# An inference step of a hybrid decoder: the MLP's instructions kept in traced order on four engines, and its last chunk widened to three pairs

## The chip, the cores and the metric

The kernel runs on one core of one Trainium2 chip. The metric is the device time of one execution, in microseconds (us). Three runs of the kernel before took 2996.69, 2999.52 and 3004.34 us; their median is 2999.52 us. The core has five engines with a queue each: TensorE (PE, matmuls; PEld is its weight load), VectorE (DVE), ScalarE (ACT), GpSimd (POOL) and SyncE (SP, which here only starts DMA transfers). ACT starts some transfers too.

## The reference

Two layers, each a mixer and then an MLP, on 1024 prompt tokens and 8 decode tokens (1032 columns), all in float32. The change touches only the MLP, which both layers run:

```python
def _conv_ffn(xn, w_up, conv_w, conv_b, w_down, conv_state):     # xn: (tokens, 1024), normed
    gpre, up = jnp.split(xn @ w_up, 2, axis=-1)                  # 2816 gate and 2816 inner columns
    full = jnp.concatenate([conv_state.astype(gpre.dtype), gpre], axis=1)
    acc = conv_b + full[:, 0:t] * conv_w[0]
    for j in range(1, CONV_W):                                   # CONV_W = 3 taps along the tokens
        acc = acc + full[:, j:j + t] * conv_w[j]
    h = jax.nn.gelu(acc) * up
    return h @ w_down, full[:, full.shape[1] - (CONV_W - 1):]
```

The result is added to the residual; the next layer (or the last norm) follows.

## The kernel before, in words

Activations lie transposed: features on 128 partitions, the 1032 token columns along the row. A float32 operand is split into a rounded high part and a low rest (`parts`, L442), and a product is three matmuls: high by high, high by low, low by high.

Both matrix products of the MLP use a Strassen-like scheme: one 2 x 2 block product needs seven block products instead of eight, with sums on both sides. `seven` (L484) runs one such round: products 0 to 6 accumulate in three double PSUM banks in the order a b c a b c b, so product 3 needs the bank of product 0 read out, product 4 that of 1, product 5 that of 2, product 6 that of 4, and product 1 of the next round that of product 6. Each product takes its weight factor from `factors` (L446): POOL forms the sums of weight blocks (L467 to L473), ACT writes the high part (L459) and a copy in PSUM (L461), DVE subtracts for the low part (L462). Four factors are kept ahead; their split tiles are four, so factor S+4 reuses the tile of factor S.

`climb` (L570) is the up-projection: 22 rounds, f = 0 to 21, each 7 products of 24 matmuls (128 x 258 columns). A round makes 128 gate and 128 inner columns. `after(i, pt)` reads out product i: ACT copies product 0 (L600), DVE reads out products 1 (L603), 2 (L612), 3 (L595), 4 (L614), 5 (L618) and 6 (L616). POOL finishes the gate row (L593, L594, L622 to L625). `convolve` then does the three taps (ACT L629, DVE L632 four times), the GELU (ACT L634, L635) and the gating (DVE L637, twice). Round f's `convolve` is called in round f+1, after product 0. `turn` splits the seven block sums of a pair of rounds (ACT L443, DVE L444, POOL L435 to L439) and stores them in DRAM (`hid`, SP L650), 11 pairs in layer 0 and 9 in layer 1. In layer 1 the last four rounds go to DRAM unsplit (`raw`), and are multiplied after the MLP.

Round 0 is special: `first` makes the split sums of the input as its products need them, and the norm's factor `rstd` is made beside it (`make_rstd`, L221).

`descend` (L681) is the down-projection. It takes the pairs in chunks: two pairs at a time, then a single pair, then two pairs. For each chunk, j = 0 to 3 runs one round of seven products, of 6 matmuls per pair, and adds them to the accumulators `big` (L714; ACT L712 in chunk 0). `load_factors` (L559) brings a chunk's pairs from `hid`, on SP for chunk 0 and on ACT later. In chunks 1 and 2, the residual `res` is loaded through one buffer `sq_t` (SP L728), scaled (POOL L729) and added (POOL L730). In the last chunk, product 0 is read out to a buffer `t` and added by POOL to three accumulators (L718), DVE scales by `rstd` (L707), and the squares for the next norm are made (ACT L736, POOL L204).

What sets the order: each engine has one queue and runs it front to back. A scheduler of the programming framework decides at build time in which order the instructions stand in each queue, from priorities and its own estimate of what is ready; it may put a later instruction of the source ahead of an earlier one.

Of the kernel before, what the change touches and what calls it, by code (L numbers as in the profile page):

```python
# [8 lines left out]
F32 = mybir.dt.float32  # L9
# [9 lines left out]
T = 1024  # L19
# [51 lines left out]
class Trunk:  # L71
# [149 lines left out]
    def make_rstd(self, bank, std=None, tmp=None):  # L221

        nc = self.nc
        tmp = self.vec.tile([128, TT], F32, name="sq_t") if tmp is None else tmp
        parts = []
# [4 lines left out]
        if std is not None:  # L230
            nc.scalar.copy(std, tmp)
        self.rsqrt(self.rstd, tmp)
        if std is not None:
            nc.gpsimd.tensor_tensor(std, std, self.rstd, op=OP.mult)

    def rsqrt(self, out, x):
# [5 lines left out]
        nc.scalar.activation(out, out, AF.Exp, scale=-0.5)  # L242
        nc.vector.tensor_tensor(x, x, out, op=OP.mult)
# [202 lines left out]
    def factors(self, srcs, kt, mixed=False):  # L446
# [6 lines left out]
        (a11, a12), (a21, a22) = ((r[:, ::2], r[:, 1::2]) if mixed else (r[:, :kt], r[:, kt:]) for r in raws)  # L453

# [11 lines left out]
        s1, s2 = (ext.tile([128, 4, 128], F32, name=x, bufs=1)[:, :kt] for x in ("s1", "s2"))  # L466
        nc.gpsimd.tensor_tensor(s1, a21, a22, op=OP.add)  # L467
        nc.gpsimd.tensor_tensor(s2, s1, a11, op=OP.subtract)
        yield parts(s2)
        yield parts(s1)  # L470
        nc.gpsimd.tensor_tensor(a11, a11, a21, op=OP.subtract)
        yield parts(a12)
        nc.gpsimd.tensor_tensor(a12, a12, s2, op=OP.subtract)  # L473
        yield parts(a11)
# [3 lines left out]
    def factor_stream(self, units):  # L478

        units = list(units)  # L480
        next(units[0])
# [5 lines left out]
    def seven(self, pp, stream, rhs, after):  # L487

        nc = self.nc
        banks = {}
        for i, x in enumerate("abcabcb"):
            while len(self.ahead) < 4:
                nxt = next(stream, None)
                if nxt is None:
                    break
                self.ahead.append(nxt)
            hi, lo = self.ahead.popleft()
            new = x not in banks  # L500
            if new:
                banks[x] = pp.tile([128, 2, 512], F32, name=f"pp{x}", bufs=1)
            pt, right = banks[x][:, :, :QW], rhs(i)
            for k, r in enumerate(right):
                for n, (w, part) in enumerate(((hi, 0), (hi, 1), (lo, 0))):
                    for q in range(2):
                        nc.tensor.matmul(pt[:, q], w[:, k], r[:, part, q, :QW], start=(new and k == 0 and n == 0),  # L507
                                         stop=(k == len(right) - 1 and n == 2), skip_group_check=True)
            after(i, pt)

    def ffn(self, l, last):
# [11 lines left out]
        chunks = [(p, p + 1) for p in range(0, NP - 3, 2)] + [(NP - 3,), (NP - 2, NP - 1)]  # L523
# [11 lines left out]
        with self.tp(name="fpp", bufs=1, space=PSUM) as pp, self.tp(name="fpm", bufs=2, space=PSUM) as self.ps:  # L535
            self.climb(l, stream, pp, right, tu, chunks, hid, raw, NP)
            self.descend(l, last, stream, pp, tu, chunks, hid)
        pools.pop().__exit__(None, None, None)
        if last:
            with self.tp(name="fin", bufs=1) as fin:  # L540
                y = [fin.tile([128, TT], F32, name=f"y{i}") for i in range(4)]
                parts = []
                for k in range(4):
                    nc.sync.dma_start(y[k], raw[k])
                    nc.gpsimd.tensor_tensor(y[k], y[k], self.rstd, op=OP.mult)
# [6 lines left out]
        if not last:  # L552
            self.open_x()
            self.order = PAIRS
            for m in PAIRS:
                nc.scalar.activation(self.xh[m], big[:, m], AF.Copy)  # L556
                nc.vector.tensor_tensor(self.xl[m], big[:, m], self.xh[m], op=OP.subtract)

# [7 lines left out]
    def climb(self, l, stream, pp, right, tmp, chunks, hid, raw, pairs):  # L566
# [12 lines left out]
        inner, tail = {}, lambda: None  # L579
# [4 lines left out]
        def up(f):  # L584
# [3 lines left out]
            c11 = x = None  # L588

            def begin():  # L590
                if f == 0:
# [1617 lines left out]
```

## Time and profile before

| | |
|---|---|
| median of 3 runs | 2999.52 us |
| profiled execution, its own time | 2999.0 us |
| its span in the trace | 2997.3 us |
| busy share of the span | PE 92%, PEld 83%, DVE 63%, ACT 46%, POOL 37% |
| mean granted TensorE clock | 0.97 of full speed |
| chain that ended last, by engine | PE 47%, DVE 16%, POOL 11%, DMA 9%, issue 8%, ACT 8% |

The span holds, in order: mixer 0 (to 879 us), MLP 0 (to 1673 us), mixer 1 (to 2174 us), MLP 1 (to 2920 us) and the tail. Busy time of PE counts a matmul to its modelled end, so neighbours overlap; what a product costs is read from the distance of two starts.

### The profile page before, as it was taken

What the parts mean: (1) busy time and instruction counts of PE and PEld (TensorE: products, weight loads), DVE (VectorE), ACT (ScalarE), POOL (GpSimd) and SP (SyncE); (2) the same over time, 40 slices, a digit from 0 to 9 for tenths busy, and PEclk for the clock granted to TensorE, in tenths of its full rate; (3) what the DMA queues carried; (4) which work ended last, traced back from release to release, by engine and by line L of the source; (5) the groups of instructions that cost most, each with busy time, mean ns of one, the idle gap of its engine ahead of it and who ended that gap; (6) DMA issues with size and microseconds to landing.
All of it is one profiled execution on the core that took longest, in us unless ns stands there. A gap on an engine that the chain in (4) does not pass through costs nothing.

```text
span 2997.3 us, 49791 instructions
## 1 busy us (share of the span) xinstructions
PE 2761.6 (92%) x19363; PEld 2480.8 (83%) x19363; DVE 1895.8 (63%) x3187; ACT 1364.4 (46%) x2653; POOL 1123.3 (37%) x1114
## 2 busy tenths in 40 slices
PE   8999999999998999988889799999989999999798
PEld 7885545877898898988789789989978898998787
DVE  6566764456557777776458744445387777764586
ACT  4344433334445555555435423324365555555344
POOL 3621234321254444444454511110534444433554
PEclk9999999998999999999899999999989999999998
DMA  6621002521122343346674212221314333357632
GB/s 180 187 60 43 22 1 71 190 92 44 44 92 82 121 143 129 119 144 247 233 233 144 51 43 59 62 76 31 106 46 144 127 121 128 123 194 253 195 92 100
DMA packets 300911, 342.68 MB, mean 114 GB/s; under 512 B 34253, under 2 KB 246324, under 8 KB 300612
## 3 DMA queue, kind: packets, MB, share of 16 engines
q1 hardware_dynamic: 269948, 238.97, 25.0%
q10 hardware_dynamic: 21000, 66.98, 6.3%
q0 software_dynamic: 9728, 33.56, 3.3%
q8 instruction: 153, 2.51, 0.3%
q14 instruction: 82, 0.67, 0.1%
HBM read 241.13 MB, written 102.50 MB: 115 GB/s over the span
## 4 chain that ended last, share of the span: by engine, by line
PE 47%; DVE 16%; POOL 11%; DMA 9%; issue 8%; ACT 8%; ACTq 0%; SPq 0%; POOLq 0%; DVEq 0%
PE ps L284 13%; PE ppb L507 4%; PE ppc L507 3%; DVE big L632 3%; DMA sq_t<-res 3%; PE ppa L507 3%; PE pp L284 2%; PE ps L1314 2%; PE pd L284 2%; POOL s L467 2%; DMA hid<-big 2%; POOL big L622 2%; PE ps L791 1%; DMA wr<-in_ffn_w_up_dram 1%; ACT ps L461 1%
## 5 line engine op out<-in xcount | busy, mean ns | idle before, releaser
L507 PE MATMUL ppb<-s,wl 128*128 128x258 f32 x2304 | 315.8, 289 | 38.3 <-DVE big L614 10.8
L507 PE MATMUL ppb<-s,wh 128*128 128x258 f32 x2304 | 310.0, 289 | 30.2 <-DVE tu L603 25.9
L507 PEld LDWEIGHTS ppb<-s,wl 128*128 128x128 f32 x2304 | 294.2, 194 | 50.1 <-ACT wl L459 28.4
L507 PEld LDWEIGHTS ppb<-s,wh 128*128 128x128 f32 x2304 | 293.4, 195 | 36.6 <-ACT big L443 27.6
L461 ACT COPY ps<-wr 128x512 f32<-128x512 f32 (+2 forms) x440 | 205.3, 468 | 137.1 <-DVE wl L462 49.1
L507 PE MATMUL ppc<-s,wh 128*128 128x258 f32 x1536 | 217.0, 295 | 53.0 <-ACT wh L459 16.4
L507 PEld LDWEIGHTS ppc<-s,wh 128*128 128x128 f32 x1536 | 202.1, 199 | 61.1 <-ACT wl L459 27.9
L632 DVE SCALAR_TENSOR_TENSOR big<-big 128x524 f32<-128x524 f32 x176 | 185.5, 1094 | 94.7 <-ACT big L629 94.7
L284 PE MATMUL ps<-xh,wh 128*128 128x344 f32 x960 | 222.2, 336 | 12.7 <-ACT xh L556 12.7
L507 PE MATMUL ppc<-s,wl 128*128 128x258 f32 x1536 | 210.1, 290 | 19.8 <-DVE big L714 7.7
L507 PE MATMUL ppa<-s,wh 128*128 128x258 f32 x1536 | 209.6, 290 | 16.2 <-ACT st L712 8.2
L507 PEld LDWEIGHTS ppc<-s,wl 128*128 128x128 f32 x1536 | 197.3, 195 | 24.7 <-ACT wl L459 9.1
L462 DVE TENSOR_TENSOR wh<-ps,wh 128x512 fp32r<-128x512 f32 (+2 forms) x308 | 166.1, 539 | 80.9 <-ACT ps L461 54.4
L284 PE MATMUL ps<-xl,wh 128*128 128x344 f32 x960 | 214.2, 326 | 1.8 <-DVE xl L187 1.8
L462 DVE TENSOR_TENSOR wl<-ps,wl 128x512 fp32r<-128x512 f32 (+2 forms) x308 | 165.8, 538 | 76.0 <-ACT ps L461 46.4
L507 PEld LDWEIGHTS ppa<-s,wh 128*128 128x128 f32 x1536 | 197.7, 196 | 19.3 <-ACT st L712 8.4
L271 POOL TENSOR_TENSOR wr<-wr,gains 128x1024 f32<-128x1024 f32 (+1 forms) x44 | 84.3, 1915 | 338.3 <-DMA wr<-in_odd_w_in_dram 196.4
L284 PE MATMUL ps<-xh,wl 128*128 128x344 f32 x960 | 210.6, 325 | 0.0
L507 PE MATMUL ppa<-s,wl 128*128 128x258 f32 x1536 | 200.7, 283 | 2.5 <-DVE wl L462 0.8
L507 PEld LDWEIGHTS ppa<-s,wl 128*128 128x128 f32 x1536 | 190.7, 190 | 4.5 <-DVE wl L462 1.2
L284 PEld LDWEIGHTS ps<-xh,wh 128*128 128x128 f32 x960 | 161.5, 190 | 19.1 <-ACT xh L556 12.9
L467 POOL TENSOR_TENSOR s<-wr 128x512 f32<-128x512 f32 (+2 forms) x88 | 90.0, 1023 | 231.5 <-ACT wh L459 93.6
(773 smaller groups left out, 6026.6 us busy)
## 6 DMA issues: line engine op xcount, KB each, us to landing
s<-hid ACTq DMA_DIRECT2D x112, 520.0 KB
wr<-in_ffn_w_up_dram SPq DMA_DIRECT2D x88, 512.0 KB
hid<-big SPq DMA_DIRECT2D x76, 520.0 KB
hid<-st SPq DMA_DIRECT2D x57, 520.0 KB
wr<-in_ffn_w_down_dram SPq DMA_DIRECT2D x80, 256.0 KB
s<-hid SPq DMA_DIRECT2D x28, 520.0 KB
wr<-in_odd_w_in_dram SPq DMA_DIRECT2D x24, 512.0 KB
wr<-in_even_w_in_dram SPq DMA_DIRECT2D x18, 512.0 KB
```

The source lines that it names most:

```text
L271: self.gain_eng.tensor_tensor(raw, raw, gain[:, :, None].to_broadcast([128, kt, m]), op=OP.mult)
L284: nc.tensor.matmul(outs[g], l[:, kw, :], r[k][:, g * GW:(g + 1) * GW], start=(n == 0 and i == 0), stop=(n == kt - 1 and i == 2))
L461: nc.scalar.copy(pt, x)
L462: nc.vector.tensor_tensor(lo, pt, hi, op=OP.subtract)
L467: nc.gpsimd.tensor_tensor(s1, a21, a22, op=OP.add)
L507: nc.tensor.matmul(pt[:, q], w[:, k], r[:, part, q, :QW], start=(new and k == 0 and n == 0), stop=(k == len(right) - 1 and n == 2), skip_g ...
L622: p.tensor_tensor(g[:, 2 + HW:2 + T], u2[:, :T - HW], self.rstd[:, HW:T], op=OP.mult)
L632: v.scalar_tensor_tensor(cv[:, c], g[:, n + c.start:n + c.stop], taps[:, at:at + 1], cv[:, c], op0=OP.mult, op1=OP.add)
L791: nc.tensor.matmul(pt, l[:, k, :], r[k][:, s], start=(k == 0 and i == 0), stop=(k == n - 1 and i == 2))
L1314: nc.tensor.matmul(po[64 * g:64 * g + 64], v[:, kb, 64 * g:64 * g + 64], p[:, g * 512:(g + 1) * 512], start=first, stop=last)
```

## The change

The MLP's instructions on PE, DVE, ACT and POOL are tied, each to the one before it on its engine in the traced (source) order, by dependencies that need no semaphore. SP is not tied. The source is laid out anew to suit: an `agenda` holds steps for each product, and `seven` runs them after the read-out (late = 0) or after the next weight factor (late = 1). Factor S+4 is made behind product S. The taps, GELU and gating of a round are spread over products 0 to 4 of the next round; the seven turns of a pair over fifteen products; the norm over round 0. POOL's first two weight sums of a unit move two products ahead. In `descend` the chunks end with one of three pairs, whose product 0 runs twice, into banks a and b, so that it is not read out alone; POOL's three adds of `t` move to the chunk before. The last chunk's third pair is loaded behind the products of the chunk before. In layer 1, `rstd` multiplies the unsplit rounds before they are stored. Cut to its core (`...` marks what is left out):

```diff
+    @contextmanager
+    def ordered(self):
+        traced = self.nc.cur_bb.bb.instructions
+        head = traced[-1]
+        yield
+        start = next(k for k in reversed(range(len(traced))) if traced[k] is head) + 1
+        queues = {x.engine: None for x in (self.nc.tensor, self.nc.vector, self.nc.scalar, self.nc.gpsimd)}
+        for i in traced[start:]:
+            if i.engine in queues:
+                if queues[i.engine] is not None:
+                    self.tc.add_manual_dep(i, queues[i.engine].name, mybir.DependencyInfo(
+                        mybir.DependencyClass.NoSync, mybir.DependencyReason.DATA), reason="order")
+                queues[i.engine] = i
...
     def factor_stream(self, units):
+        for _ in range(2):
+            next(units[0])
         for i, u in enumerate(units):
-            if i + 1 < len(units):
-                next(units[i + 1])
-            yield from u
+            for n in range(7):
+                if i + 1 < len(units) and n in (0, 5):
+                    next(units[i + 1])
+                yield next(u)
...
+        self.fill(stream)
         for i, x in enumerate("abcabcb"):
...
-            after(i, pt)
+            after(i, banks[x][:, :, :QW])
+            for step in self.agenda.pop((self.step, 0), ()):
+                step()
+            self.fill(stream)
+            for step in self.agenda.pop((self.step, 1), ()):
+                step()
+            self.step += 1
...
-        chunks = [(p, p + 1) for p in range(0, NP - 3, 2)] + [(NP - 3,), (NP - 2, NP - 1)]
+        chunks = [(p, p + 1) for p in range(0, NP - 3, 2)] + [(NP - 3, NP - 2, NP - 1)]
...
+            s, wide = self.step + 7, f < NF - 1
+            self.plan(s, 1, first_tap)
+            for n in (1, 2):
+                for h, c in enumerate((slice(0, n3 // 2), slice(n3 // 2, n3))):
+                    self.plan(s + n if wide else s + 2 * n - 1 + h, 0, lambda n=n, c=c: tap(n, c))
+            self.plan(s + (3 if wide else 5), 0, gelu)
+            for h, c in enumerate((slice(0, HW), slice(HW, TT))):
+                self.plan(s + (4 if wide else 6 + h), 0, lambda c=c: gate(c))
+            if f >= 2 * pairs:
+                self.plan(s + (4 if wide else 8), 0, keep)
+            if f % 2 and f < 2 * pairs:
+                for i, n in enumerate((5, 7, 9, 11, 12, 13, 14) if wide else (10, 12, 14, 16, 17, 18, 19)):
+                    self.plan(s + n, 1, lambda i=i: turn(f, i))
...
         def first(i):
-            for n in ((0,), (1,), (2, 4), (), (3,), (6,), (5,))[i]:
+            for n in ((0,), (1,), (2, 4), (3,), (), (6,), (5,))[i]:
                 for j in range(4):
-                    self.parts(right[4 * MADE[n] + j], self.sums(n, xs[j], p if j < 3 and n < 4 else v))
+                    self.sums(n, xs[j], p if j < (2 if n == 1 else 3) else v)
+                for j in range(4):
+                    self.parts(right[4 * MADE[n] + j], self.halves(xs[j][(0, 0, 2, 1, 0, 2, 3)[n]]))
...
-                    else:
+                    elif to_go or i:
                         v.tensor_tensor(self.halves(to), pt, self.halves(to), op=OP.add)
-                    if end:
-                        if i < 3:
-                            x = (a22, a12, a21)[i]
-                            p.tensor_tensor(x, x, t, op=OP.add)
+                    if to_go == 1 and i < 3:
+                        x = (a22, a12, a21)[i]
+                        p.tensor_tensor(x, x, t, op=OP.add)
+                    if to_go == 1 and j == 3:
+                        self.load_factors(chunks[-1][2], 14 * (c % 2), hid, (i,), nc.scalar)
...
-                self.seven(pp, stream, lambda i: [self.down[x, i] for x in chunk], after)
+                self.seven(pp, stream, lambda i: [self.down[x, i] for x in chunk], after, not to_go)
```

## Rows read from the trace of the kernel before

**Rows 1.** Windows of MLP 0: length, busy (count) of PE, PEld, DVE, ACT, POOL; clock; DMA.

```profile
879.39:923.88 44.49, 33.12 (x185) 29.06 (x183) 42.14 (x54) 27.23 (x45) 15.68 (x14) 0.81 0.13 40
...
923.88:1394.15 470.27, 431.29 (x3526) 425.94 (x3525) 344.01 (x471) 264.88 (x450) 209.56 (x251) 1.00 0.40 137
1394.50:1453.08 58.58, 45.66 (x339) 43.45 (x337) 26.50 (x54) 33.28 (x85) 21.85 (x27) 0.91 0.77 275
1453.08:1557.89 104.81, 91.51 (x674) 89.07 (x673) 56.29 (x111) 38.52 (x113) 57.02 (x59) 0.90 0.67 223
...
1600.87:1672.84 71.97, 65.62 (x506) 62.19 (x504) 63.18 (x125) 39.13 (x113) 52.03 (x47) 1.00 0.26 71
```

**Rows 2.** Windows of MLP 1, same columns, without round 0:

```profile
2218.10:2691.55 473.45, 437.20 (x3525) 430.88 (x3524) 339.06 (x464) 261.16 (x443) 203.41 (x246) 0.99 0.39 131
2691.90:2739.67 47.77, 44.15 (x339) 42.15 (x337) 21.53 (x47) 29.95 (x78) 16.05 (x18) 0.96 0.79 269
2739.67:2850.32 110.65, 90.95 (x674) 87.81 (x673) 55.48 (x111) 37.56 (x113) 55.77 (x59) 0.92 0.64 215
2850.32:2920.30 69.98, 65.87 (x506) 63.11 (x504) 63.03 (x124) 33.44 (x108) 39.88 (x45) 0.98 0.27 83
```

**Rows 3.** Waits of PE, 923 to 1394 us: in total, times, longest.

```profile
PE ppb L507 <- DVE tu L603: 12.5, 10, 1.8
PE ppc L507 <- DVE big L612: 7.6, 5, 1.9
...
PE ppb L507 <- DVE sq_t L614: 6.0, 5, 1.2
```

**Rows 4.** Timeline of PE, two products: start us, us, engine line op:

```profile
982.63 3.04 PE L507 MATMUL ppc<-s,wl 128*128 128x258 f32 x24
985.51 3.04 PE L507 MATMUL ppb<-s,wh 128*128 128x258 f32 x24
```

**Rows 5.** Timeline of DVE between the taps and a late read-out:

```profile
1108.68 3.68 DVE L632 SCALAR_TENSOR_TENSOR big<-big 128x524 f32<-128x524 f32 x3
...
1114.77 0.69 DVE L603 TENSOR_TENSOR tu<-ppb,tu 128x516 f32<-128x516 f32 x1
```

**Rows 6.** DVE by line and form, 940 to 1390 us: busy, mean ns, idle before.

```profile
L632 DVE SCALAR_TENSOR_TENSOR big<-big 128x524 f32<-128x524 f32 x80 | 87.2, 1129 | 45.9 <-ACT big L629 45.9
L462 DVE TENSOR_TENSOR wh<-ps,wh 128x512 fp32r<-128x512 f32 x69 | 47.3, 686 | 12.2 <-ACT wh L459 12.1
```

**Rows 7.** ACT by line and form, 940 to 1390 us:

```profile
L461 ACT COPY ps<-wr 128x512 f32<-128x512 f32 x99 | 57.9, 585 | 47.6 <-DVE wl L462 17.1 <-POOL wr L473 15.5 <-POOL big L593 7.9
L459 ACT ACTIVATE wh<-wr 128x512 fp32r<-128x512 f32 x50 | 31.3, 625 | 0.0
...
L634 ACT ACTIVATE big<-big 128x1024 f32<-128x1024 f32 x20 | 21.2, 1061 | 26.9 <-DVE big L632 26.9
...
L635 ACT ACTIVATE big<-big 128x8 f32<-128x8 f32 x20 | 3.9, 195 | 0.0
```

**Rows 8.** The taps by source line, 940 to 1390 us: duration min, median, max.

```profile
L632 DVE SCALAR_TENSOR_TENSOR big<-big x80: 749/906/1804, 945.6 to 1379.3; 128x524 f32<-128x524 f32 x80
```

**Rows 9.** Timeline of ACT just after PE's first MLP matmul at 879.39 us:

```profile
880.61 0.61 ACT L459 ACTIVATE wh<-wr 128x512 fp32r<-128x512 f32 x1
881.13 0.61 ACT L459 ACTIVATE wl<-s 128x512 fp32r<-128x512 f32 x1
```

**Rows 10.** Waits of POOL, 1453 to 1558 us: in total, times, longest.

```profile
POOL sq_t L729 <- DMA sq_t<-res: 27.9, 12, 5.0
```

**Rows 11.** POOL by line and form, 1453 to 1558 us:

```profile
L729 POOL TENSOR_TENSOR sq_t<-sq_t,std 128x516 f32<-128x516 f32 x13 | 16.8, 1293 | 27.9 <-DMA sq_t<-res 27.9
```

**Rows 12.** Timeline of PE: a product of chunk 1; the first matmul after MLP 0.

```profile
1475.36 2.95 PE L507 MATMUL ppc<-s,wl 128*128 128x258 f32 x12 [3.53 <-ACT wl L459]
...
1685.50 1.23 PE L284 MATMUL ps<-xh,wh 128*128 128x344 f32 x3 [12.66 <-ACT xh L556]
```

**Rows 13.** Timeline of POOL after MLP 1:

```profile
2923.39 11.38 POOL L545 TENSOR_TENSOR y<-y,rstd 128x1032 f32<-128x1032 f32 x4 [5.93 <-DMA y<-raw]
```

More of the change, by code (lines that the diff above doesn't have):

```diff
@@ L491, in seven @@
+    def seven(self, pp, stream, rhs, after, twice=False):
         nc = self.nc
         banks = {}
+        self.fill(stream)
         for i, x in enumerate("abcabcb"):
[L494 to L498, printed above, removed]
-            hi, lo = self.ahead.popleft()
-            new = x not in banks
-            if new:
-                banks[x] = pp.tile([128, 2, 512], F32, name=f"pp{x}", bufs=1)
@@ L503, in seven @@
[L503 to L508, printed above, removed]
-            after(i, pt)
+            hi, lo = self.ahead.popleft()
@@ new lines, in seven @@
+            right = rhs(i)
+            for y in "ab" if twice and i == 0 else x:
+                new = y not in banks
+                if new:
+                    banks[y] = pp.tile([128, 2, 512], F32, name=f"pp{y}", bufs=1)
+                pt = banks[y][:, :, :QW]
+                for k, r in enumerate(right):
+                    for n, (w, part) in enumerate(((hi, 0), (hi, 1), (lo, 0))):
+                        for q in range(2):
+                            nc.tensor.matmul(pt[:, q], w[:, k], r[:, part, q, :QW], start=(new and k == 0 and n == 0),
+                                             stop=(k == len(right) - 1 and n == 2), skip_group_check=True)
@@ new lines, in climb, with norm @@
+        tmp = self.st.bitcast(F32).rearrange("p a q w -> p (a q w)")[:, :TT]
+        sums = {}
+        def norm(i):
+            if i in (2, 3, 4):
+                s = slice((i - 2) * GW, (i - 1) * GW)
+                v.tensor_scalar(tmp[:, s], sums.pop(i - 1), 1.0 / DM, EPS, op0=OP.mult, op1=OP.add)
+            if i in (1, 2, 3):
+                sums[i] = self.bank()[:, :GW]
+                nc.tensor.matmul(sums[i], self.ones, self.sq[:, (i - 1) * GW:i * GW], start=True, stop=True)
+            if i == 4:
+                nc.scalar.copy(self.std, tmp)
+                self.rsqrt(self.rstd, tmp, False)
+                sums["rows"] = self.vec.tile([128, TT], F32, name="sq")[:, :512].rearrange("p (i f) -> p i f", i=4)
+                self.conv_rows(l, sums["rows"])
+            if i == 6:
+                self.newton(self.rstd, tmp)
+                p.tensor_tensor(self.std, self.std, self.rstd, op=OP.mult)
+                self.conv_setup(taps, sts, sums["rows"])
@@ L730, in after, with conv_rows @@
                         p.tensor_tensor(big[:, m, s], big[:, m, s], x, op=OP.add)
-                self.seven(pp, stream, lambda i: [self.down[x, i] for x in chunk], after)
-                while late:
-                    scale()
-                for m in (j, j + 4) if end and not last else ():
-                    x = self.slot(14 * (1 - c % 2) + 2 * (squares % 4)).bitcast(F32).rearrange("p a q w -> p (a q w)")[:, :TT]
-                    nc.scalar.activation(x, big[:, m], AF.Square)
-                    self.add_sq(x, squares)
-                    squares += 1
-    def conv_setup(self, l, taps, st, rows):
+                self.seven(pp, stream, lambda i: [self.down[x, i] for x in chunk], after, not to_go)
+        while late:
+            scale()
+    def conv_rows(self, l, rows):
         nc, a = self.nc, self.a
```

195 lines of the change are left out of this document (110 added, 85 removed).

## The prediction

> **What bounds the kernel now.** I read the stages by windows first, then PE's waits in each, then the timelines around a wait. In both MLPs the granted clock is full in rounds 1 to 21 and the matmul engine is never out of work for long: PE is busy 431.3 of 470.3 us [rows 1]. The reader is to see that PE nevertheless isn't at its own pace. Two products that follow each other without a wait start 2.88 us apart [rows 4], so a round of seven costs 20.16 us and rounds 1 to 21 cost 423.4 us; they take 470.3 and 473.5 us [rows 1, 2]. The missing 47 and 50 us are short waits. PE's waits there are seven groups, 39.4 us in sum, nearly all on three read-outs of DVE: products 1, 2 and 4 (L603, L612, L614), 29 times, 1.2 to 1.9 us at the longest [rows 3]. The timeline says why: DVE stands in the taps, then waits for the GELU, gates, and only then reads out product 1 [rows 5]. DVE idles 45.9 us before the taps alone [rows 6]. So it isn't short of time (344 of 470 us busy [rows 1]); its queue has the work in a bad order.
>
> In `descend` a product of two pairs is 12 matmuls, half of the above: 1.44 us, 10.08 us per round, 40.3 us per chunk. Chunk 0 takes 58.6 and 47.8 us, chunks 1 and 2 together 104.8 and 110.7 us against 80.6 [rows 1, 2]. In chunks 1 and 2, POOL waits 27.9 us for `res` loads [rows 10], and the weight factors stand behind that: PE waits 3.5 us for one, and the product after such a wait takes 2.95 us instead of 1.44, at a granted clock of 0.90 in this stage [rows 12, 1].
>
> **Rounds 1 to 21.** The new order puts read-out S first in DVE's slot S, two taps each in slots 1 and 2, the GELU in ACT's slot 3 ahead of the weight factor, the gating in slot 4. The one tight chain starts at the end of product 1 and must have read out product 4 before product 6 starts, 4 products or 11.52 us later: read-out 0.69, two taps 2.26, low part of a turn 0.69, low weight part 0.69, read-out 2 0.69, two taps 2.26 [rows 6], GELU 1.06 + 0.20, factor 0.63 + 0.59 on ACT [rows 7], low weight part 0.69, read-out 4 0.69: 11.1 us (read-outs and low parts taken at the 0.69 of rows 5 and 6). It fits by 0.4 us, less than the spread of the taps (0.75 to 1.80 us, mean 1.13 [rows 8, 6]). I therefore charge 0.25 us a round; the bounds are 0 and, with two of the four taps at their longest, 1.6 - 0.4 = about 1 us (2 x 0.67 more, and 0.25). The other read-outs have two products or more of slack. Over a pair of rounds DVE's work is about 34 us of 40.3. The turns' stores block ACT for about 1 us at most, and factors are three products ahead, so nothing of it reaches PE; if that cover went, a store's wait would come straight onto a product. 42 rounds of 20.41 us are 857.2 against 943.7 us: **-86.5 us** (bounds -97 and -55).
>
> The Trainium skill, "SBUF — State Buffer", section "Who interferes with whom", speaks against the layout: a DVE instruction with two inputs in SBUF contends with a GpSimd one that reads SBUF, and whoever starts later is held up entirely. The taps' range in [rows 8] agrees with it. The new source traces POOL's two weight sums beside the first two taps; by the rule those would go to their longest while the others go to the shortest: 2 x 1.80 + 2 x 0.75 = 5.1 instead of 4.5 us a round, 25 us in all.
>
> **Round 0.** ACT's queue now begins with four weight factors. Two of them need tiles that the mixer's last projection holds until PE's first MLP matmul starts; before, ACT made these only at 880.6 and 881.1 us, with the input's split ahead of them [rows 9]. Now the split of product 0 waits behind them: 2 x (0.63 + 0.59) [rows 7], then one split on ACT and DVE, 0.63 + 0.69: product 0 starts 3.7 us late. Later splits queue behind the read-out of the product before, and six POOL sums of 1.29 us [rows 11] still stand before product 2. Followed through, round 1 starts some 6.6 us later than before, on 44.5 [rows 1]: **+13.2 us** for both layers (bounds 0, if the splits overlap as now, and +24, if each of four splits exposes another 4 x 0.69). The norm's Newton steps are off the path; only their three DVE passes are late, in round 1, whose read-outs have a product of slack.
>
> **Chunk 0.** Its loads on SP come before those of chunk 1 on ACT, which the old order let in early, so products wait less for transfers. Layer 0 still turns the last pair here through two buffers that must be stored first, and ACT stands behind each store. I keep half of the loss, rounded: 46 us, and 44 in layer 1, which has no turn here: **-16.4 us** (bounds -26, no wait, and 0).
>
> **Chunks 1 and 2.** The chain load, scale, add, next load runs through one buffer, twice per j; a scale and an add are 2 x 1.29 us [rows 11]. One j takes 104.8 / 8 = 13.1 us, so a load with its handover is (13.1 - 5.2) / 2 = 4.0 us (5.0 the longest [rows 10]). The change leaves the chain, but POOL now runs in source order: between the second add and the next scale come three weight factors on ACT and two weight sums, 4.1 us in which the load may run but the scale may not start, and the last weight sum of a unit waits for the whole pair. ACT stands behind it, DVE behind ACT, and PE at product 5. I get 13.9 us per j: 111 us in layer 0. In layer 1, chunk 2 is the chunk before the last and gets the three adds of `t`, 3.9 us per j of which half is covered: 119 us. Together **+14.6 us** (bounds: PE's pace, -54; 3 us more per j, +63).
>
> **Last chunk.** The old single-pair and two-pair chunks took 72.0 and 70.0 us [rows 1, 2]. The new one has 28 products of 18 matmuls and four more of 18 for the doubled product 0: 32 x 2.16 = 69.1 us of PE, DVE loses 32 read-outs, so nothing else should bind: 70 us, **-2 us** (bounds -4 and +6).
>
> **Ends.** After MLP 0, PE waited 12.7 us [rows 12]: the last squares needed DVE and POOL before the next operand could be written. Now two squares come after the first operands, the last accumulators need two read-outs' time: I take 4.7 us left, **-8 us** (bounds -11 and -2). After MLP 1, POOL's four scalings, 11.4 us, fed PE one by one [rows 13]; these go into the climb, where POOL is under half busy. The load still has to land: **-5 us** (bounds -8 and 0).
>
> The sum is -86.5 + 13.2 - 16.4 + 14.6 - 2 - 8 - 5 = -90.1 us on the profiled execution's own 2999.0 us (span 2997.3, median of the runs 2999.5, so no correction): **2909 us**.
>
> **Rivals.** (1) *Chunks 1 and 2 come down to PE's pace and round 0 costs nothing.* POOL scales and adds early, since neither depends on product 6; then they take about 87 us per layer: 2909 - 24 - 32 - 13 = 2840 us. For: the loads' wait is only 27.9 of 104.8 us; against: one buffer still serves all. (2) *Head-of-line blocking is dearer*: each load takes the longest 5.0 us, 2 us more per j in 16, and round 0 exposes one split more per layer: 2909 + 32 + 6 = 2947 us. For: ACT's loads of the next chunk now start just when the second `res` load does. (3) *The GELU takes the place of the old wait*: in each round ACT's factor stands behind the GELU, DVE's low part behind the factor, the read-out of product 4 behind that, and PE's product 6 behind all. With all four taps at 1.80 us the chain is 2.7 us longer and stalls 2.3 us a round on top of my 0.25: 2909 + 42 x 2.3 = 3006 us. The gain of the whole change is gone from 2.4 us a round, that is from 1.67 us a tap. For: the margin is 0.4 us; against: the mean tap is 1.13 us and three of four stood beside POOL already. (4) *The port lock alone*, by the taps' rows at their ends, 0.6 us a round: 2934 us.
>
> **How the numbers follow.** The forecast gets 0.55 (2875 to 2940), rival 1 0.15, rival 2 0.18, rival 3 0.07, rival 4 0.05. Two in ten lie outside 2862 to 2960: most of rival 1 and all of rival 3. A measurement of this kernel tells about 0.3%, 9 us, from no change. Slower is rival 3 but for its mild form, 0.05; no change 0.02; faster the rest, 0.93.
>
> **What would show it.** Right: rounds 1 to 21 near 428 us each with read-out waits of products 1 and 2 gone and at most a small one before product 6; first products of round 0 some 3 to 4 us later; chunks 1 and 2 still waiting for `res`, through a weight factor; one last chunk near 70 us; 5 us or less before the next mixer's first matmul. Wrong: waits of 2 us before product 6 in every round, DVE's low parts waiting for ACT's copy behind the GELU; chunks 1 and 2 below 100 us; round 0 shorter than 44 us.

## The result and the profile after

The changed kernel takes 2971.35 us, median of 4 runs (2967.24 to 2972.0), beside 3001.11 us (2996.69 to 3004.34) for the kernel before: ratio 0.9899, interval 0.9882 to 0.9916. That is 30 us faster; 90 were forecast, and the time lies above the range. The profiled execution has a span of 2965.5 us against 2997.3.

The first two lines below are the page of the changed kernel: busy time by engine, and the chain that ended last by engine. They look like a success: PE was 47% of that chain before and is 78% now. A chain summed over the span doesn't show that one stage grew.

```profile
PE 2753.7 (93%) x19507; PEld 2496.5 (84%) x19507; DVE 1819.4 (61%) x3060; ACT 1334.1 (45%) x2543; POOL 1126.0 (38%) x1088
...
PE 78%; DVE 8%; POOL 4%; DMA 4%; ACT 3%; issue 2%; ACTq 0%; DVEq 0%; SPq 0%; POOLq 0%
```

Windows of the changed kernel, columns as in [rows 1]: MLP 0 by round 0, rounds 1 to 21, chunk 0, chunks 1 and 2, chunk 3, last chunk; then MLP 1 in the same way, which has no chunk 3.

```profile
879.56:947.62 68.06, 36.80 (x180) 31.95 (x179) 44.27 (x53) 32.15 (x54) 22.54 (x14) 0.67 0.09 27
947.62:1373.75 426.13, 423.40 (x3531) 423.23 (x3530) 331.98 (x471) 255.65 (x446) 221.87 (x257) 1.00 0.42 144
1373.75:1437.63 63.88, 47.68 (x343) 46.53 (x342) 29.30 (x59) 35.45 (x88) 18.53 (x30) 0.87 0.83 294
1437.63:1554.93 117.30, 91.18 (x674) 89.79 (x673) 57.19 (x111) 37.69 (x113) 60.04 (x61) 0.88 0.57 195
1554.93:1605.17 50.24, 42.42 (x339) 42.20 (x337) 29.67 (x56) 19.75 (x56) 31.31 (x31) 0.93 0.68 230
1605.17:1674.05 68.88, 68.88 (x579) 68.88 (x577) 41.83 (x66) 32.73 (x60) 28.94 (x22) 1.00 0.24 70
...
2167.60:2236.34 68.74, 37.40 (x179) 33.02 (x179) 44.53 (x53) 32.30 (x54) 22.52 (x14) 0.68 0.08 27
2236.34:2663.74 427.40, 424.95 (x3530) 424.78 (x3529) 330.45 (x468) 253.54 (x442) 221.86 (x255) 1.00 0.42 146
2663.74:2708.58 44.84, 42.40 (x342) 42.23 (x341) 22.86 (x47) 30.47 (x78) 15.82 (x21) 0.96 0.78 271
2708.58:2826.32 117.74, 89.63 (x674) 87.71 (x673) 57.34 (x111) 38.32 (x113) 75.01 (x73) 0.89 0.62 218
2826.32:2895.40 69.08, 69.08 (x577) 69.03 (x576) 38.91 (x63) 23.64 (x52) 18.82 (x17) 1.00 0.18 57
```

Two windows of the kernel before that [rows 1, 2] leave out, chunk 3 of layer 0 and round 0 of layer 1:

```profile
1557.89:1600.87 42.98, 41.26 (x338) 40.51 (x337) 27.88 (x55) 18.84 (x56) 16.51 (x22) 1.00 0.73 238
...
2173.61:2218.10 44.49, 32.83 (x185) 28.59 (x183) 42.13 (x54) 27.15 (x45) 15.68 (x14) 0.81 0.13 40
```

The differences, layer 0 and layer 1. "Ends" runs from the end of one MLP to the start of the next, and from the last MLP to the end of the span:

| stage | forecast | measured |
|---|---|---|
| rounds 1 to 21 | -86.5 | -44.1 - 46.1 = -90.2 |
| round 0 | +13.2 (0 to +24) | +23.6 + 24.2 = **+47.8** |
| chunk 0 | -16.4 (-26 to 0) | +5.3 - 2.9 = **+2.4** |
| chunks 1 and 2 | +14.6 | +12.5 + 7.1 = +19.6 |
| chunk 3, layer 0 | 0 | +7.3 |
| last chunk | -2 | -3.1 - 0.9 = -4.0 |
| ends | -13 | -7.2 - 6.9 = -14.1 |

They sum to -31.2; the span changed by -31.8, since the windows of the kernel before leave out 0.35 us a layer between round 21 and chunk 0. So the steps for rounds 1 to 21, the last chunk and the ends were right to a few us. Of the 59 us that are missing, round 0 has 34.6 and chunk 0 18.8.

**Rounds 1 to 21.** PE's waits there are one row, where [rows 3] shows read-outs of three products:

```profile
PE ppb L534 <- DVE sq L660: 2.7, 1, 2.7
```

**Round 0.** DVE does the work it did before (44.3 us busy, 42.1 in [rows 1]), but in 68.1 us instead of 44.5: it used to be busy 95% of the time and is now 65%. The granted clock fell from 0.81 to 0.67. DVE's timeline in the changed kernel shows where it stands:

```profile
872.38 0.69 DVE L467 TENSOR_TENSOR wh<-ps,wh 128x512 fp32r<-128x512 f32 x1 [2.04 <-ACT ps L466]
879.80 1.30 DVE L416 TENSOR_TENSOR rstd<-pp,rstd 128x688 f32<-128x688 f32 x2 [6.74 <-PE pp L285]
...
883.16 0.69 DVE L467 TENSOR_TENSOR wh<-ps,wh 128x512 fp32r<-128x512 f32 x1 [1.46 <-ACT ps L466]
883.76 4.66 DVE L445 TENSOR_TENSOR s<-big,s 128x516 fp32r<-128x516 f32 x3
...
898.58 2.51 DVE L445 TENSOR_TENSOR s<-big,s 128x516 fp32r<-128x516 f32 x4
904.46 0.70 DVE L648 TENSOR_TENSOR tu<-ppb,tu 128x516 f32<-128x516 f32 x1 [3.37 <-PE ppb L534]
```

Two things are to be seen. From 873 to 880 us DVE has nothing, since its queue holds weight parts (L467) ahead of the first split (L445). ACT, which writes each part first, stands before its third, whose tile the out-projection's matmuls read to their end:

```profile
879.75 0.63 ACT L464 ACTIVATE wl<-s 128x512 fp32r<-128x512 f32 x1 [6.13 <-PE pp L285]
```

And at 901 us DVE waits for PE to finish product 1, since the read-out (L648) stands ahead of product 2's splits, for which PE will then wait. PE's waits in this window, three of six rows:

```profile
PE ppc L534 <- ACT s L444: 12.9, 2, 7.3
PE ppc L534 <- DVE s L445: 4.1, 1, 4.1
PE ppa L534 <- ACT s L444: 4.0, 1, 4.0
```

All six sum to 31.0 us, each a wait for a split; 4.0 of them lie before product 0. In the kernel before PE's waits in round 0 are 11.3 us.

**Chunks 1 and 2.** One of PE's waits of 6 to 7 us at product 5, followed back through four engines in the changed kernel (POOL, ACT, DVE, PE):

```profile
1509.31 1.27 POOL L827 TENSOR_TENSOR sq_t<-sq_t,std 128x516 f32<-128x516 f32 x1 [6.39 <-DMA sq_t<-res]
...
1511.89 0.72 POOL L476 TENSOR_TENSOR wr<-wr,s 128x256 f32<-128x256 f32 x1
```
```profile
1512.65 0.42 ACT L464 ACTIVATE wl<-wr 128x256 fp32r<-128x256 f32 x1 [9.20 <-POOL wr L476]
```
```profile
1513.37 0.42 DVE L467 TENSOR_TENSOR wl<-ps,wl 128x256 fp32r<-128x256 f32 x1 [8.86 <-ACT ps L466]
1513.71 0.69 DVE L810 TENSOR_TENSOR big<-ppc,big 128x516 f32<-128x516 f32 x1
```
```profile
1514.54 2.92 PE L534 MATMUL ppc<-s,wl 128*128 128x258 f32 x12 [6.60 <-DVE big L810]
```

POOL waits for the residual's load. A weight sum stands behind it, ACT's weight part behind the sum, DVE's behind ACT's, and behind DVE's part the read-out of product 2, whose bank product 5 needs.

### The profile page after: what moved, and what is told of

It is laid out like the page before. It is cut to its first block, busy times and chain, and to the rows that moved or that the text cites. A ratio compares the mean times of both kernels' runs of the same rounds, so it can differ in the third digit from the quotient of the medians.

```text
span 2965.5 us, 49527 instructions
## 1 busy us (share of the span) xinstructions
PE 2753.7 (93%) x19507; PEld 2496.5 (84%) x19507; DVE 1819.4 (61%) x3060; ACT 1334.1 (45%) x2543; POOL 1126.0 (38%) x1088
## 4 chain that ended last, share of the span: by engine, by line
PE 78%; DVE 8%; POOL 4%; DMA 4%; ACT 3%; issue 2%; ACTq 0%; DVEq 0%; SPq 0%; POOLq 0%
PE ppb L534 16%; PE ps L285 13%; PE ppc L534 11%; PE ppa L534 10%; PE pp L285 6%; PE ps L1410 2%; PE pd L285 2%; DMA sq_t<-res 2%; PE ps L887 2%; PE pd L1319 1%; POOL big L828 1%; PE ps L1167 1%; PE pd L1385 1%; PE ps L1155 1%; PE pd L1386 1%
## 5 line engine op out<-in xcount | busy, mean ns | idle before, releaser
L534 PEld LDWEIGHTS ppb<-s,wh 128*128 128x128 f32 x2376 | 303.3, 196 | 18.2 <-ACT ps L466 6.2
L534 PEld LDWEIGHTS ppb<-s,wl 128*128 128x128 f32 x2376 | 300.4, 194 | 12.1 <-ACT s L444 4.1
L467 DVE TENSOR_TENSOR wh<-ps,wh 128x512 fp32r<-128x512 f32 (+2 forms) x280 | 162.4, 580 | 181.9 <-ACT ps L466 179.6
L534 PEld LDWEIGHTS ppc<-s,wh 128*128 128x128 f32 x1536 | 202.8, 202 | 50.2 <-ACT ps L466 18.0
L467 DVE TENSOR_TENSOR wl<-ps,wl 128x512 fp32r<-128x512 f32 (+2 forms) x280 | 161.9, 578 | 131.0 <-ACT ps L466 129.3
L534 PE MATMUL ppa<-s,wl 128*128 128x258 f32 x1536 | 204.4, 287 | 14.1 <-ACT s L444 8.1
L534 PE MATMUL ppa<-s,wh 128*128 128x258 f32 x1536 | 200.8, 285 | 8.2 <-ACT tu L808 8.2
L466 ACT COPY ps<-wr 128x512 f32<-128x512 f32 (+2 forms) x400 | 198.5, 496 | 2.8 <-DVE st L734 1.8
L464 ACT ACTIVATE wh<-wr 128x512 fp32r<-128x512 f32 (+2 forms) x200 | 108.6, 543 | 176.2 <-PE ppb L534 69.5
L464 ACT ACTIVATE wl<-wr 128x512 fp32r<-128x512 f32 (+2 forms) x200 | 108.6, 543 | 170.6 <-PE ppb L534 60.0
L472 POOL TENSOR_TENSOR wr<-wr,wr 128x512 f32<-128x512 f32 (+2 forms) x80 | 94.3, 1179 | 230.3 <-ACT ps L466 230.2
```

The lines of the kernel that those rows point to most:

```text
L464: nc.scalar.activation(hi, x, AF.Copy)
L466: nc.scalar.copy(pt, x)
L467: nc.vector.tensor_tensor(lo, pt, hi, op=OP.subtract)
```

## The experiments

Ratios are to the kernel before, run beside each on the same chip. "Round 0" is, from PE's timeline, the time from the out-projection's last matmul to the first of round 1; the changed kernel has 67.9 and 68.6 us (layer 0, layer 1), the kernel before 44.3 in both. Where TensorE is free, products of rounds 0 and 1 interleave and that mark is a rough one. A second mark is the bulk of round 1's product 3: in layer 0 it starts 47.0 us after the out-projection in e1 and e6, 73.8 in e5 and 76.6 in the changed kernel.

| | ratio (interval) | round 0, us |
|---|---|---|
| e1 tie from round 1 on | 0.9695 (0.9672 to 0.9718) | 37.8, 38.7 |
| e2 no tie | 0.9872 (0.9847 to 0.9898) | - |
| e3 residual's load ahead | 0.9659 (0.9632 to 0.9687) | 69.1, 68.0 |
| e4 splits one product ahead | 0.9839 (0.9812 to 0.9865) | 56.9, 58.0 |
| e5 TensorE free in round 0 | 0.9889 (0.9864 to 0.9913) | 55.7, 56.3 |
| e6 only TensorE tied in round 0 | 0.9715 (0.9692 to 0.9738) | 38.3, 40.2 |
| e7 chunk 0's loads on ACT | 0.9915 (0.9891 to 0.9939) | 67.8, 67.9 |
| e8 e1, e3 and e7 | 0.9489 (0.9459 to 0.9519) | 37.8, 38.0 |
| e9 last three pairs in two chunks | 0.9954 (0.9937 to 0.9971) | - |
| e10 before, tied | 1.0527 (1.0475 to 1.0579) | - |
| e11 splits two products ahead | 0.9830 (0.9797 to 0.9863) | 56.8, 55.9 |
| e12 e1, e3, loads spread | 0.9489 (0.9452 to 0.9525) | 37.8, 37.8 |
| e13 e11, first splits before parts | 0.9772 (0.9741 to 0.9804) | 49.2, 48.4 |
| e14 product 0's splits before parts | 0.9890 (0.9859 to 0.9922) | 63.4, 64.2 |
| e15 e13 and e3 | 0.9546 (0.9515 to 0.9576) | 49.3, 48.4 |
| e16 e1 and e3 | 0.9480 (0.9451 to 0.9510) | 37.8, 37.8 |

### Tie or layout: e1, e2, e10

e1 begins the chain of `ordered` behind round 0; e2 has no chain; e10 puts the chain around the two calls in the kernel before.

```
+        head = self.mark        # e1: set in climb after f == 0
-        for i in traced[start:]:
+        for i in ():            # e2
```

> The tie (each engine's instructions held in traced order) begins only behind round 0 of each MLP; the layout is unchanged. Theory A: the 23.6 and 24.2 us that round 0 lost are the tie's: the splits of the next product stand in ACT's and DVE's queues behind read-outs, weight parts and the norm's steps that are late. Then round 0 is 44 to 50 us instead of 68.1 and 68.7, everything behind it as in the changed kernel, and the time is about 2925 us (2971 - 46), range 2915 to 2940. Rival B: round 0 is long by its layout (more sums on POOL beside DVE's splits, the norm's steps spread over products 1 to 6), whatever the order: round 0 stays at 65 to 70 us and the time at 2965 to 2975 us.

> The layout alone: no engine is held to traced order anywhere. Theory A for round 0: 44 to 50 us, as with the tie from round 1 on. For rounds 1 to 21 two readings stand against each other. If the tie carries the 44 and 46 us won there, they go back towards 470 us each and the time is about 3015 us (2971 - 46 + 90). If the laying out of the steps product by product carries them, they stay near 427 us and the time is 2915 to 2940 us, as with the tie from round 1 on.

> The kernel before with the tie alone: its own layout, in which the taps, the GELU and the gate of a tile are traced in one lump inside product 0 of the next round and the splits behind read-outs. Theory: the tie is worth something only on steps laid out product by product; a lump in DVE's and ACT's queues now stands ahead of the read-outs of products 1 to 3, PE waits 4 us or more a round for them, and the time is 3050 to 3250 us. Rival: the tie itself brings the gain of rounds 1 to 21 whatever the layout, and the time is 2950 to 2990 us.

e1 came to 2907.8 us beside 2997.9, below theory A's range even: untying round 0 wins 30 us in each layer, since with the new layout an untied round 0 takes 38 us, 6 less than before the change. Rival B falls: the layout of round 0 is a gain, the tie is the loss. e2 answers the question on rounds 1 to 21: without a tie the climb (round 0 to 21, PE's timeline) takes 510 and 506 us, against 494 and 496 in the changed kernel, and 466 and 467 in e1. So on this layout the tie carries the gain of rounds 1 to 21, and the layout alone (-1.3%) wins as much as layout and tie together (-1.0%), within the intervals. e2's total, 2962 us, missed both expectations: the climbs lose 26 us against the changed kernel, and the untied chunks 0 to 3 of layer 0 win 25, 206 us instead of 231. There the tie costs too (in layer 1 little: 159.5 us untied, 162.6 tied). e10 shows the reverse, +5.3%: in every second round of the old order, tied, the read-out of product 1 stands behind a lump of taps, GELU and gate. Its rounds 1 to 21 now take 499 and 495 us, and its round 0 takes 78.8 and 78.2, some 34 more than untied: in round 0 the tie costs in the old layout as well. Its row of PE's waits for rounds 1 to 21 of layer 0:

```profile
PE ppb L523 <- DVE tu L620: 45.3, 11, 4.4
```

### Which queue in round 0: e5, e6

```
+            if i.engine in queues and (k >= body or i.engine != self.nc.tensor.engine):   # e5; e6: ==
```

> Untying round 0 won 64 us, 26 us of it in each round 0. Which queue does it? Here round 0 is tied on DVE, ACT and POOL and TensorE alone is free; behind round 0 all four are tied. Theory F (splits stand late in the in-order queues of ACT, DVE and POOL, so TensorE has nothing to multiply whatever its own order): round 0 stays at 55 to 66 us and the time at 2945 to 2972 us. Rival G (TensorE itself stands behind the first late operand while another product's operands are there, as its interleaving of products in the untied round 0 suggests): round 0 is 38 to 45 us and the time 2907 to 2925 us.

> The mirror: round 0 is tied on TensorE alone, and DVE, ACT and POOL are free there. Theory F: round 0 is 38 to 46 us and the time 2907 to 2928 us. Rival G: round 0 stays at 58 to 66 us and the time at 2950 to 2972 us. In between, both orders share it.

Theory F. With only TensorE tied, round 0 is 38.3 us at 95% DVE (36.25 of 38.32 below), in the very order of products that took 68. With TensorE free and the others tied the total is the changed kernel's within the interval; its round 0 looks shorter only because round 1's products are mixed in (the climb is 493 us, as tied, and the second mark moves by 2.8 us). The window of e6's round 0:

```profile
884.35:922.67 38.32, 26.47 (x178) 24.79 (x178) 36.25 (x44) 26.36 (x45) 19.87 (x13) 0.78 0.15 48
```

### What stands ahead of the splits: e4, e11, e14, e13

```
+        near = deque(rhs(i) for i in range(2))      # e13: ahead of the fill; e11: behind it; e14: rhs(0) alone, ahead
         self.fill(stream)
 ...
+            if i < 5:
+                near.append(rhs(i + 2))             # e11, e13; e4 has rhs(i + 1); e14 has no lead
             after(i, banks[x][:, :, :QW])
```

> Tied as the changed kernel, but in round 0 the sums and splits of product i+1 are traced ahead of the read-out of product i and of the weight parts that follow it, instead of behind them. Theory A says that what stands ahead of the splits in the queues is what costs: round 0 shrinks by 8 to 15 us in each layer and the time is 2940 to 2957 us. Rival B (POOL and DVE slow each other on the sums and splits, and the amount of work sets the pace): round 0 stays within 4 us of 68 and the time is 2963 to 2975 us.

> Tied as the changed kernel from the first product on, but in round 0 the sums and splits of product i+2 are traced ahead of the read-out of product i (in the changed kernel they stand behind the read-out of product i+1; one product ahead took 11 us off round 0). Theory F: in the changed kernel product, read-out and next split run one after the other, round a ring through TensorE; a lead of two products opens the ring, round 0 is 44 to 50 us in each layer and the time 2925 to 2938 us. Rival J: what is left after a lead of one is the norm (its square root on ACT stands ahead of the splits of product 5, a wait of 5.4 us) and POOL's sums, so round 0 stays at 51 to 56 us and the time at 2943 to 2952 us.

> Tied as the changed kernel, with the splits of product 0 alone traced ahead of the first weight parts and no lead behind it. Theory K: the head start is worth its 10 to 14 us by itself, round 0 is 54 to 59 us instead of 68 and the time is 0.980 to 0.984 of before. Rival M (without a lead the ring of product, read-out and split sets the pace from product 1 on, and an early product 0 only waits there): round 0 falls by under 5 us and the time is 0.986 of before or more.

> Tied from the first product on as the changed kernel, splits two products ahead of the read-outs as in the run before, and now the sums and splits of products 0 and 1 are traced ahead of the first weight parts as well. With TensorE alone tied, the first splits began at 870 us, 10 us before round 0; in the changed kernel DVE stands at its second weight part from 873 to 880 us, since that part's PSUM bank is still the out-projection's, and begins its first split at 883.8. Theory K: that lost head start is the part of round 0 that a lead of two products left (53 us against 38); then round 0 is 38 to 46 us in each layer and the time 0.969 to 0.976 of before (2908 to 2928 us on the first chip). Rival L (POOL's sums, 1.6 to 1.7 us each beside DVE's splits, pace the products whatever their start): round 0 stays at 50 to 55 us and the time at 0.979 of before or more.

A lead of one product gives 11 us a layer, as theory A said; a lead of two no more, against theory F and for rival J. Both of J's reasons show in e11's timelines, the norm's at another place than J said: ACT waits 4.9 us for POOL's sums before a split of product 2, and after product 6 PE waits 3.5 us for a weight part that stands behind the norm's square root on ACT. The early splits alone (e14) give 4.5 us: product 0 then starts at once, and PE stands 6.1 us before product 1 (rival M). Both together (e13, where product 1's splits are early too) give 19 to 20, more than their sum of 16 to 17. Counted from the MLP's own first matmul, as the expectation did, e13's round 0 is 44.6 and 43.8 us: theory K, with a total just above its range. (K's text puts DVE's stand from 873 to 880 us down to a PSUM bank; by ACT's row at 879.75 above it is the weight part's tile.) DVE's timeline in e13 shows the head start, 20 us ahead of the 883.8 of the changed kernel:

```profile
863.81 4.62 DVE L445 TENSOR_TENSOR s<-big,s 128x516 fp32r<-128x516 f32 x2
...
881.29 2.51 DVE L445 TENSOR_TENSOR s<-big,s 128x516 fp32r<-128x516 f32 x4
```

So two thirds of the 30 us are shown to be the traced places of the splits: behind read-outs, which make PE, read-out and split a ring, and behind weight parts whose tile the out-projection holds. The last 8 to 11 us between e13 and e6 are not tested. PE's timeline in e13 has two waits that e6's has not:

```profile
882.62 1.23 PE L535 MATMUL ppa<-s,wl 128*128 128x258 f32 x4 [4.58 <-ACT wl L464]
...
926.57 0.41 PE L848 MATMUL ps<-ident,sq 88*128 88x88 f32 x1 [3.51 <-DVE wl L467]
```

The first weight part now stands behind product 1's splits on ACT, and the part at 926 us behind the norm's square root. ACT also waits 8.8 us for POOL's sums in that round, so rival L isn't excluded for a part of it.

### The residual's load: e3

```
+                    if c in (1, 2) and i == 0:
+                        held[j] = self.vec.tile([128, TT], F32, name=("sq_t", "sq")[j % 2])
+                        nc.sync.dma_start(held[j], self.res[j + c * 4 - 4])
 ...
-                        x = self.vec.tile([128, TT], F32, name="sq_t")[:, s]
-                        nc.sync.dma_start(x, self.res[m][:, s])
+                        x = held[j][:, s]
```

> Tied as the changed kernel, but in chunks 1 and 2 the residual's load starts at product 0 of its round into one of two buffers used in turn, in place of two halves loaded at product 6 into one buffer; its two multiplies and two adds on POOL stand where they stood. Theory C: POOL's wait for that load (41.8 us over layer 0's chunks, 29.3 over layer 1's) stands in front of the weight sums, so ACT's weight parts, DVE's read-outs and PE follow it: the waits of 6 to 8 us at product 5 go, chunks 1 and 2 take 85 to 100 us instead of 117.3 and 95 to 105 instead of 117.7, chunk 3 of layer 0 about 43 instead of 50.2, and the time is 2915 to 2940 us. Rival D: POOL's own work (4 residual steps of 1.28 us, weight sums of 2.9, and in layer 1's chunk 2 three adds more) or the transfers (11.7 MB a chunk) set the pace: the chunks change by under 5 us each and the time is 2960 to 2975 us.

Theory C, and beyond its range: 2896.7 us. Chunks 1 and 2 come within 3 to 5 us of PE's pace (80.6 us) at full clock, with POOL's work unchanged (60.2 and 73.4 us busy), so rival D falls. The edit does three things at once: a second buffer, a load six products earlier, and one load in place of two halves; which of them is needed isn't told apart. Windows of e3, chunks 1 and 2 of each layer:

```profile
1439.30:1522.60 83.30, 81.97 (x675) 80.92 (x674) 58.78 (x111) 38.49 (x113) 60.16 (x61) 1.00 0.77 269
2670.10:2755.70 85.60, 82.01 (x675) 80.97 (x674) 57.65 (x109) 38.45 (x112) 73.43 (x71) 1.00 0.83 289
```

Chunk 3 of layer 0 falls from 50.2 to 41.5 us. Chunk 0 of layer 1 grows from 44.8 to 49.4: SP's queue holds the second residual's load until its tile is free, and the weight loads behind it start 25.2 us into the chunk instead of 20.3 (read from SP's timelines, not tested).

### Chunk 0 of layer 0: e7, e12

```
-  self.load_factors(c, n, hid, range(2 * i, min(2 * i + 2, 7)), nc.sync)     # for i < 4
+  self.load_factors(c, n, hid, range(2 * i, min(2 * i + 2, 7)), nc.scalar)   # e7
+  self.load_factors(c, n, hid, (i,), nc.sync)                                # e12, for all i
```

> Tied as the changed kernel, but the 14 loads of 520 KB for chunk 0 are issued on ACT's queue instead of SP's, where the stores of pairs 9 and 10 stand behind them. Theory H (the store waits its turn behind the loads in one queue): ACT's 7.9 us wait for the store of st goes, PE's 8.2 us wait with it, chunk 0 of layer 0 takes 54 to 58 us instead of 63.9, and the time is 2958 to 2966 us. Rival I (7.3 MB at about 400 GB/s are 18 us whatever the queue, or ACT now stands behind an issue that waits for a free slot): chunk 0 stays at 62 to 68 us and the time at 2968 to 2980 us.

> The tie from round 1 on, the residual's load ahead, and chunk 0's loads on SP's queue at one index (two loads of 520 KB) a product over all seven products of round 21, in place of two indices a product over the first four. The first two add to 2971 - 64 - 75 = 2832 us. If the store of pair 9 then no longer stands behind 5 MB of loads, chunk 0 of layer 0 falls from 64 to 55 to 60 us and the time is 2822 to 2832 us. If the last indices now come late for product 5 or 6 of chunk 0, it is 2833 to 2842 us.

e7 goes rival I's way by its second reason: on ACT's queue chunk 0 falls to 59.0 us, but ACT now stands 4.7 us before a GELU behind an issue, and rounds 1 to 21 grow by 9.1 and 5.6 us: nothing won. e12 misses both of its ranges (0.9489 is about 2847 us on the first chip): spread over seven products, chunk 0 is 65.4 us. So neither change of the queue shortens this place as a whole, and around it the DMA engines are full: in e12 they are busy all the time from 1352 to 1385 us (share 1.00). That the bytes set the pace is read from this; no run moves fewer of them. GB/s in 40 slices of e12 from 1345 to 1385 us, and the window:

```profile
GB/s 0 0 112 233 345 412 358 399 424 337 391 283 324 295 333 341 266 254 358 391 343 400 413 408 416 408 416 420 412 416 420 358 362 183 266 316 404 408 424 381
...
1352.00:1385.00 33.00, 21.59 (x167) 21.11 (x166) 18.02 (x30) 14.43 (x32) 8.02 (x10) 0.81 1.00 363
```

### The last chunk: e9

```
-        ... + [(NP - 3, NP - 2, NP - 1)]
+        ... + [(NP - 3,), (NP - 2, NP - 1)]
```

> Tied and laid out as the changed kernel, but the last three pairs are a chunk of one pair and a chunk of two again, with product 0 of the last in two banks as in the changed kernel. A product of one pair is 6 matmuls, some 0.72 us, and each needs a weight part and a read-out on DVE: if DVE sets the pace of that chunk, the last three pairs take 72 to 76 us instead of 68.9 and 69.1 and the time is 2975 to 2988 us. Rival: the merged chunk won nothing, TensorE sets the pace either way, and the time is 2966 to 2974 us.

0.9954 against 0.9899: the merged chunk is worth about 0.55%, 16 us, give or take 7 by the intervals. In layer 0 the last three pairs take 28.2 + 48.6 = 76.8 us instead of 68.9, in layer 1 84.7 instead of 69.1, where PE waits 9.2 us once for a weight part. The chunks just before them are shorter, though, by 5.0 and 9.8 us, so from chunk 1 on the two descents are 9 us longer, not 16. In layer 0 DVE is busy 79% of the single-pair chunk, and PE waits 3.6 us there for its read-outs; the transfers are at a share of 0.93 as well, so which of them binds isn't told apart.

```profile
1624.70:1652.89 28.19, 22.88 (x170) 20.98 (x169) 22.36 (x53) 12.74 (x54) 21.89 (x27) 1.00 0.93 320
1652.89:1701.49 48.60, 46.70 (x388) 46.29 (x387) 38.36 (x66) 26.33 (x62) 28.20 (x27) 1.00 0.15 35
```

### Together: e8, e15, e16

> The tie from round 1 on, the residual's load ahead, and chunk 0's loads on ACT's queue, together. If the three costs lie in different stages they add: 2971 - 64 - 75 - 8 = 2824 us, range 2815 to 2835. If the loads of a chunk, no longer covered by waits, come late (11.7 MB in a chunk of 41 us), chunks 1 and 2 are back at 47 us or more each and the time is 2845 us or more.

> The kernel of the splits ahead of parts and read-outs, tied throughout, with the residual's load ahead. If the costs lie in different stages they add: round 0 at 38 to 46 us, chunks 1 and 2 at 83 to 86 us together, and the time is 0.944 to 0.953 of before. If round 0 stays at 50 us or more (rival L) it is 0.955 or more.

> The tie from round 1 on and the residual's load ahead, nothing else. The sum of the two alone, against the changed kernel's 0.990 of before: 0.9695 + 0.9659 - 0.9899 = 0.9455 of before, some 2835 us. If something joins the two (chunk 0 of layer 1 was 4.6 us longer with the residual's load ahead) it is 0.949 to 0.952.

e16 has the lowest ratio, 0.9480 (2840.6 us beside 2996.1), within the intervals of e8 and e12. Its round 0 and its chunks add up as in e1 and e3; what joins the two is chunk 0 of layer 1, 49.5 us against 43.1 in e1. e8 and e12 are no faster, as e7 and e12's chunk 0 say. e8 lies in its second range (2847 us on the first chip) by luck: that range wanted slow chunks 1 and 2, and they take 83.3 and 85.9 us. e15, tied throughout, has e13's round 0 and comes to 0.9546, just above its range. Windows of e16, layer 0, as in the first block above but without the last chunk:

```profile
878.75:916.55 37.80, 29.01 (x196) 26.02 (x195) 36.59 (x44) 26.49 (x45) 20.18 (x13) 0.86 0.15 48
916.55:1344.31 427.76, 423.31 (x3514) 422.76 (x3513) 330.57 (x471) 255.39 (x445) 220.62 (x255) 1.00 0.41 143
1344.31:1409.10 64.79, 47.39 (x343) 46.15 (x342) 29.12 (x59) 35.40 (x88) 18.23 (x30) 0.84 0.86 302
1409.10:1492.40 83.30, 81.98 (x675) 80.93 (x674) 58.73 (x111) 38.57 (x113) 60.12 (x61) 1.00 0.77 269
```

## Why the prediction was wrong, point by point

- **Rounds 1 to 21: right** (428.6 us a layer forecast, 426.1 and 427.4 measured). The chain fits: taps have a mean of 784 ns now against 1111 before, over the whole stretch, so rival 3 has no ground. (Two figures of the prediction were off here: the bound's 1.6 - 0.4 is 1.2 us a round, which gives -47 and not -55, and the gain would be gone from 1.77 us a tap, not 1.67. Neither was reached.) The Trainium skill, "SBUF — State Buffer", section "Who interferes with whom", would have added 25 us here by the taps; no such time shows, since the weight sums are over as the taps begin (in the round at 1116 us POOL's two sums end at 1118.77 and DVE's first tap starts at 1118.46). DVE and POOL side by side are slow even so: two of the gates' three groups (L686), which now lie beside POOL's sums, went from 694 and 692 to 1117 and 1322 ns. The slow pairs moved from work on the chain to work with slack. In round 0 a split takes 0.63 us alone and 1.55 beside POOL's sums (the rows at 898.58 and 883.76), while POOL's sums go from 1.30 to 1.6 to 2.1. Two stretches of the timelines, DVE's and then POOL's:

```profile
888.35 2.32 DVE L205 TENSOR_TENSOR sq<-sq,rstd 128x1032 f32<-128x1032 f32 x1
890.59 1.76 DVE L445 TENSOR_TENSOR s<-big,s 128x516 fp32r<-128x516 f32 x1
```
```profile
887.83 1.74 POOL L436 TENSOR_TENSOR big<-big 128x516 f32<-128x516 f32 x1
889.65 2.14 POOL L437 TENSOR_TENSOR big<-big 128x516 f32<-128x516 f32 x1
```

  They fit turns: DVE's end at 890.67 and 892.35 us, 1.1 and 0.6 after POOL's ends at 889.57 and 891.79, and POOL's second end lies 1.1 after DVE's first. So each is held up by the other in turn, and the Trainium skill's section, by which whoever starts later is held up, agrees with these rows.
- **Round 0: the step that failed.** I charged 3.7 us for the late first split and 6.6 for all, bounded by four exposed splits at full speed. The 3.7 held: PE waits 4.0 us before product 0. What failed is the rest, 2.9 us for all later splits: PE waits 27 us for those, where all its waits in round 0 were 11.3 before. The missing thought is in [rows 1]: DVE was busy 42.14 of 44.49 us there. A stage whose work fills an engine keeps its time only while that engine never stands; in traced order it stands whenever PE's product, its read-out and the next split follow one another, and the splits that used to run beside the out-projection come after it. The row was there to read, in DVE's timeline of the kernel before, whose MLP starts on PE at 879.39 us [rows 1]: 10.3 us of splits on DVE are done by 873.4.

```profile
862.95 7.04 DVE L444 TENSOR_TENSOR s<-big,s 128x516 fp32r<-128x516 f32 x3 [3.53 <-ACT s L443]
870.14 3.28 DVE L444 TENSOR_TENSOR s<-big,s 128x516 fp32r<-128x516 f32 x2 [0.15 <-ACT s L443]
```

  Idle DVE grew from 2.4 to 23.8 us. PE then runs slowly as well: two products next to each other are at 2.88 us at full clock, and the clock here was 0.67. Rival 2 named the place but priced one split.
- **Chunk 0: wrong, beyond its bound.** The step that failed is "products wait less for transfers": it didn't hold in layer 0, where the share of DMA in the stage was 0.77 and 275 GB/s already in [rows 1]. It is 0.83 and 294 now, and stores of the turned pair wait among the loads (ACT waits 7.9 us for one). Neither e7 nor e12 won this time back, so what would is open. Layer 1 came to 44.8 us, where 44 was forecast.
- **Chunks 1 and 2: mechanism right, size 5 us short.** POOL waits 34.3 us for `res` instead of 27.9 [rows 10], and PE 24.4 us at product 5. The same wait runs over into chunk 3 of layer 0, which I had left out (+7.3). Rival 1's time for these chunks (87 us) can be had, but not in this kernel: e3, with the load ahead into a second buffer, has 83.3 and 85.6.
- **Last chunk and ends: right**, -4.0 and -14.1 us against -2 and -13.

## What to carry to other kernels

Holding every engine to the written order pays where the order was laid out for a steady pace, and costs where a stage is filled by one engine's work or starts before the last one ends: lay out the first round with a lead, or leave it untied. Before a queue is put in order, list for each instruction that waits for a transfer what stands behind it; a load with one buffer, behind which other engines' work is queued, is worth an earlier start into a second buffer (e3 did both at once). Price a stage by its fullest engine's idle time, not by the single delay that comes to mind.

## What the runs showed that was not expected

The layout alone and the layout with the tie end within 0.3% of each other (e2, 0.9872; changed kernel, 0.9899), while the tie is worth 1.8% beyond the layout when it begins a round later (e1, 0.9695). And the wait for one load of 258 KB cost 2.4% of the kernel (e3 against the changed kernel), at eight products 5 where PE's timelines show 3.7 to 8.2 us: each such wait was followed by a product at 2.9 us instead of 1.6, and the granted clock of the stage went from 0.88 to 1.00 when the waits were gone.
